# Parked parts, per-pair activation parts and a reversed second half in three down projections

## The chip, the cores and the metric

The kernel runs on one core of a Trainium2 chip. The engines that matter are TensorE (PE, matrix products; its weight loads are a row of their own), VectorE (DVE, elementwise work), ScalarE (ACT, copies and activation functions), GpSimd (POOL) and SyncE (SP). SP and POOL issue transfers between the device memory (HBM) and the on-chip memory (SBUF); 16 DMA engines carry them. Matrix products accumulate in eight PSUM banks of 128 x 512 fp32. The metric is the device time of one execution in microseconds, the median of several runs. The kernel before takes 2493.71 us (three runs, 2493.4 to 2493.81).

## What is computed

A trunk of two post-norm layers on x of 256 positions and 2048 features, all in float32. Each sub-layer is `x <- LayerNorm(ALPHA * x + sublayer(x))`.

1. A gated MLP (gMLP): `z = gelu(x @ w_in)` with 2 x 6144 columns, halves u and v; v is normalised, mixed over positions in 128-wide windows by masked 128 x 128 matrices, and `(u * s) @ w_out` projects 6144 back to 2048. This last product is the first down projection.
2. A gated feed-forward block: `h = x @ w_up` with 2 x 5504 columns, a causal width-3 convolution, `silu(g) * a`, then `@ w_down` from 5504 to 2048: the second down projection.
3. Latent attention (MLA) with 16 heads, low-rank query and key/value, rotary keys, and an output product.
4. A second feed-forward block, as 2: the third down projection.

## The kernel before

**Numbers and splits.** An fp32 product is made of three products in fp32r. A tensor x becomes a high part (ACT's rounding copy) and a low part (DVE's subtraction), and `prod_b` issues high x high, low x high and high x low, each a matmul of 512 columns on a 128 x 128 weight tile. `prod_a` does the same in the up and gate stages with the weights on the other side.

**The stream of weights.** `Feed` holds one list of chunks, in the order in which PE uses them: 48 chunks of the v stage, 48 of the gate stage u, the first down projection, the first up stage, and so on. A chunk is 128 x 2048 fp32 (1.05 MB). `Feed._load` issues its load on SP's queue into a slot `raw`; `Feed._split` makes the parts `wh` and `wl`. `Feed.next` hands out a chunk and first issues the splits of two chunks ahead and the loads of four. All of these, the activations, the residual and the parts live in one pool `big` of 22 slots of 8 KB per partition; a load waits until its slot is released. The order of the instructions on each engine is set when the program is built, by a scheduler that issues each as soon as it expects its inputs; afterwards every engine works through its list in order.

**Eight and seven products.** In the v stage and the down projections a chunk is a unit of two k (two 128-row blocks of the contraction) by 1024 output columns, and x has two blocks of 128 positions: a 2 x 2 by 2 x 2 block product. `Banks.eight` forms it as eight block products. `Banks.seven` forms it in the manner of Strassen and Winograd as seven, from sums of weight blocks (`ts`, split to `th`, `tl`, by `Feed._seven`) and sums of activation blocks (`combine`). Four of the eight banks (`q3`, `p2`, `e`, `q4`, called DIRECT) take direct terms; the other four (OWN) are joined by `Banks.rest` after the last seven of a half and added to the residual by `Norm.fold`; `Norm.piece` adds DIRECT.

**A down projection.** `down` goes twice over all k, once for each half of the 2048 output columns. `BACK` lists which units take seven products (7 of 24 in each half of the first down projection, 6 of 22 in the others) and the order of the second half. The activations' parts are made four k at a time by `Sums.quad`, and the sums of a seven by `Sums.make`. The last units of the second half are held back (`late`) and worked off in `boundary`, between the parts of the layer norm. The residual occupies two slots throughout; `Norm.restore` brings it back to its scaled form during the next up stage from rows that `Norm.rows` loads.

**Stages in time.** v up to 257 us of the profiled execution, u to 549, the first down projection to about 803, the first up stage to 1285, its down projection to about 1511, attention to about 1773, the second up stage to 2255, and the last down projection to the end. In an up stage a group is four chunks and two pairs of columns; its epilogue (`conv`, `pair`) runs on ACT and DVE while PE is at the next group.

Of the kernel before, what the change touches and what calls it, by code (L numbers as in the profile page):

```python
# [15 lines left out]
P = 128  # L16
# [32 lines left out]
V_PAIRS = [[0, 1, 2, 3, 4, 5, 6, 7]] + [[2, 0, 3, 1, 4, 5, 6, 7]] * 5  # L49
V_SEVEN = [()] + [(2, 3, 4, 6)] * 5  # L50

# [8 lines left out]
def halves(n_k):  # L60

    one = [tuple(range(k, min(k + 2, n_k))) for k in range(0, n_k, 2)]
    two = []
    for q in BACK[n_k][1]:
        two += one[2 * q : 2 * q + 2][:: -1 if q in BACK[n_k][2] else 1]
    return [one, two]


class Feed:
# [3 lines left out]
    def __init__(self, nc, pool, chunks):  # L73
        self.nc, self.pool, self.chunks = nc, pool, chunks
        self.raw, self.parts = {}, {}
        self.loaded = self.split = self.used = 0

    def _load(self):
        ap, cols = self.chunks[self.loaded][:2]
# [14 lines left out]
    def _split(self):  # L94
        i = self.split
        cols, kind = self.chunks[i][1:]
# [36 lines left out]

    def ahead(self, n_load, n_split):
# [15 lines left out]
def trunk(ctx: ExitStack, tc: tile.TileContext, x, xT, gm_in, gm_wout, ffn_up, ffn_dn,  # L150
# [7 lines left out]
    ps = ctx.enter_context(tc.tile_pool(name="ps", bufs=8, space=bass.MemoryType.PSUM))  # L158

# [10 lines left out]
    chunks = []  # L170
# [6 lines left out]
    def back(w, n_k):  # L177

        for hf, units in enumerate(halves(n_k)):
            c = slice(hf * 1024, (hf + 1) * 1024)  # L180
            for u in units:
                if len(u) == 1:
                    chunks.append((w[u[0], :, c], 1024, "wide"))
                else:
                    chunks.append((w[u[0] : u[0] + 2, :, c].rearrange("k p c -> p k c"), 2048,
                                   "seven" if u[0] in BACK[n_k][0] else "wide"))

# [11 lines left out]
    feed = Feed(nc, big, chunks)  # L199

    idle = cpool.tile([P, 512], BF16, name="idle")
# [6 lines left out]

    def combine(name, o, k1, k2):


        t = tp.tile([P, 4, P], F32, tag="t2", name=f"xs{name}", bufs=6)
        b0, b1 = slice(0, P), slice(P, S)
        nc.vector.tensor_tensor(t[:, 0], k1[:, b1], k2[:, b1], ALU.subtract)
        nc.vector.tensor_tensor(t[:, 1], t[:, 0], k1[:, b0], ALU.subtract)
        nc.vector.tensor_tensor(t[:, 2], k1[:, b0], k1[:, b1], ALU.subtract)
        nc.vector.tensor_tensor(t[:, 3], k2[:, b0], t[:, 1], ALU.add)
# [3 lines left out]
        return [(o[:, 0, i], o[:, 1, i]) for i in range(4)]  # L221
# [40 lines left out]
    ones = cpool.tile([P, P], F32, name="ones")  # L262
    nc.gpsimd.memset(ones, 1.0)
# [45 lines left out]
    def sum_halves(acc, name):  # L309
        lo = tp.tile([P, S], F32, tag="t1", name=f"lo_{name}", bufs=8)  # L310
        nc.scalar.copy(lo, acc[:, S : 2 * S])  # L311
        h = tp.tile([P, S], F32, tag="t1", name=f"h_{name}", bufs=8)
# [3 lines left out]
    def split_act(src, name):  # L316

        t = tp.tile([P, 2 * S], F32R, tag="t2", name=name, bufs=6)
# [11 lines left out]
    class Banks:  # L330
# [17 lines left out]
        def seven(self, a, sums, wh, wl, th, tl):  # L348
            s1, s2, s3, s4 = sums
            self.to("p1", a[0][0], wh, wl, 0)  # L350
            self.to("q5", s1, th, tl, 0)
            self.to("p7", s3, th, tl, 512)
            self.to("p6", s2, th, tl, 1024)
            self.to("q3", s4, wh, wl, 512)
            self.to("p2", a[0][1], wh, wl, 1024)
            self.to("q4", a[1][1], th, tl, 1536)

        def rest(self):

            acc = self.acc  # L360
            p1, u2, u3, w, d = [tp.tile([P, 512], F32, tag="t2", name=f"{self.tag}{n}", bufs=6)
# [5 lines left out]
            nc.vector.tensor_tensor(d, w, acc["p7"], ALU.subtract)  # L367
            return w, p1, d, u3

    class Sums:  # L370

# [786 lines left out]
```

## Time and profile before

| | |
|---|---|
| median of three runs | 2493.71 us |
| the profiled execution, its own time | 2493.04 us |
| its span | 2491.3 us |
| PE busy | 2475.7 us (99%), 13028 matmuls with transposes |
| DVE busy | 1908.8 us (77%) |
| ACT busy | 1388.8 us (56%) |
| granted TensorE clock | 0.999 |
| moved by DMA | 480.27 MB, mean 193 GB/s |

The page of the profile gives busy times by engine, DMA queues, the chain of waits that ended last and the costliest groups of instructions. In a group row stand the line, the engine, the operation, what it writes and reads, its shape and count, then busy time and the mean of one in ns, then the idle time of the engine just before and what ended it. In a row by windows stand the stretch, the busy time and count of PE, its weight loads, DVE, ACT and POOL, the granted clock, the DMA share and GB/s. In a row of waits stand the engine and line that waited, the one that ended it, the total in us, how often and the longest.

### The profile page before, as it was taken

What the parts mean: (1) busy time and instruction counts of PE and PEld (TensorE: products, weight loads), DVE (VectorE), ACT (ScalarE), POOL (GpSimd) and SP (SyncE); (2) the same over time, 40 slices, a digit from 0 to 9 for tenths busy, and PEclk for the clock granted to TensorE, in tenths of its full rate; (3) what the DMA queues carried; (4) which work ended last, traced back from release to release, by engine and by line L of the source; (5) the groups of instructions that cost most, each with busy time, mean ns of one, the idle gap of its engine ahead of it and who ended that gap; (6) DMA issues with size and microseconds to landing.
All of it is one profiled execution on the core that took longest, in us unless ns stands there. A gap on an engine that the chain in (4) does not pass through costs nothing.

```text
span 2491.3 us, 32651 instructions
## 1 busy us (share of the span) xinstructions
PE 2475.7 (99%) x13028; PEld 2128.3 (85%) x13028; DVE 1908.8 (77%) x2553; ACT 1388.8 (56%) x1891; POOL 2.9 (0%) x17
## 2 busy tenths in 40 slices
PE   9999999999999999999999999999999999999998
PEld 7888888888888888888888888988888888888886
DVE  7999866678888777666778997866487676669897
ACT  6566544445565755554655566565565555546553
POOL 0000000000000000000000000000000000000000
PEclk9999999999999999999999999999999999999999
DMA  7555554555566655555546674444465455555554
GB/s 295 198 187 214 196 186 157 181 196 194 186 217 222 223 186 200 188 184 185 187 155 201 219 247 169 168 153 168 156 231 191 169 202 182 180 179 179 209 192 181
DMA packets 86456, 480.27 MB, mean 193 GB/s; under 512 B 7712, under 2 KB 8480, under 8 KB 46752
## 3 DMA queue, kind: packets, MB, share of 16 engines
q1 hardware_dynamic: 86304, 478.19, 54.4%
q8 instruction: 102, 1.67, 0.3%
q14 instruction: 50, 0.41, 0.1%
HBM read 476.07 MB, written 2.10 MB: 192 GB/s over the span
## 4 chain that ended last, share of the span: by engine, by line
PE 96%; DVE 2%; issue 1%; DMA 1%; ACT 0%; SPq 0%; DVEq 0%; ACTq 0%
PE up L167 37%; PE u L167 11%; PE dn_q L167 9%; PE dn_p L167 6%; PE wo_q L167 4%; PE v_q L167 4%; PE mo L167 4%; PE dn_e L167 3%; PE v_p L167 3%; PE wo_p L167 3%; PE upf L167 2%; PE wo_e L167 2%; PE v_e L167 1%; PE mkv L167 1%; PE kn L167 1%; PE mq L167 1%
## 5 line engine op out<-in xcount | busy, mean ns | idle before, releaser
L108 DVE TENSOR_TENSOR wl<-raw,wh 128x1024 fp32r<-128x1024 f32 (+3 forms) x651 | 899.8, 1407 | 158.6 <-ACT wh L107 115.5
L107 ACT CAST wh<-raw 128x1024 fp32r<-128x1024 f32 (+3 forms) x651 | 761.8, 1201 | 284.9 <-DVE wl L108 120.4
L167 PE MATMUL up<-xhl,wh 128*128 128x512 f32 x2624 | 611.0, 390 | 0.0
L167 PEld LDWEIGHTS up<-xhl,wh 128*128 128x128 f32 x2624 | 487.4, 188 | 97.8
L167 PEld LDWEIGHTS up<-xhl,wl 128*128 128x128 f32 x2624 | 325.8, 192 | 6.4
L167 PE MATMUL up<-xhl,wl 128*128 128x256 f32 x2624 | 328.1, 283 | 0.0
L115 ACT CAST th<-ts 128x1536 fp32r<-128x1536 f32 x116 | 121.1, 1051 | 118.6 <-DVE ts L122 103.9
L167 PE MATMUL u<-xhl,wh 128*128 128x512 f32 x768 | 183.8, 393 | 0.3 <-DVE h_u L313 0.2
L167 PEld LDWEIGHTS u<-xhl,wh 128*128 128x128 f32 x768 | 141.3, 188 | 30.8 <-PE s L167 2.1
L116 DVE TENSOR_TENSOR tl<-ts,th 128x1536 fp32r<-128x1536 f32 x116 | 138.6, 1219 | 5.3 <-ACT th L115 4.5
L115 ACT CAST wh<-raw 128x1536 fp32r<-128x1536 f32 x58 | 85.9, 1480 | 43.2 <-DMA raw<-in_ffn_dn_dram 15.2
L116 DVE TENSOR_TENSOR wl<-raw,wh 128x1536 fp32r<-128x1536 f32 x58 | 101.6, 1752 | 5.4 <-ACT wh L115 5.4
L167 PEld LDWEIGHTS u<-xhl,wl 128*128 128x128 f32 x768 | 95.6, 192 | 2.0
L167 PE MATMUL u<-xhl,wl 128*128 128x256 f32 x768 | 96.7, 283 | 0.0
L167 PE MATMUL mo<-wh,oT 128*128 128x512 f32 x256 | 82.9, 404 | 0.0
L122 DVE TENSOR_TENSOR ts<-ts,raw 128x512 f32<-128x512 f32 x116 | 79.8, 688 | 1.8
L167 PE MATMUL wo_q<-wh,woa 128*128 128x512 f32 x256 | 78.8, 389 | 0.0
L122 DVE TENSOR_TENSOR ts<-raw 128x1024 f32<-128x1024 f32 x58 | 70.8, 1220 | 4.6 <-PE u L167 1.6
L313 DVE TENSOR_TENSOR h_0a<-up,lo_0a 128x256 f32<-128x256 f32 x41 | 17.3, 421 | 72.7 <-ACT lo_0a L311 72.7
L313 DVE TENSOR_TENSOR h_1a<-up,lo_1a 128x256 f32<-128x256 f32 x41 | 17.3, 421 | 71.9 <-ACT lo_1a L311 71.9
L167 PE MATMUL dn_q<-wh,dn0a 128*128 128x512 f32 x232 | 71.7, 390 | 0.0
L167 PE MATMUL dn_q<-wh,dn1a 128*128 128x512 f32 x232 | 71.5, 389 | 0.0
(497 smaller groups left out, 3924.6 us busy)
## 6 DMA issues: line engine op xcount, KB each, us to landing
raw<-in_ffn_up_dram SPq DMA_DIRECT2D x172, 1024.0 KB, 4.7
raw<-in_gm_in_dram SPq DMA_DIRECT2D x93, 1024.0 KB, 4.7
raw<-in_ffn_dn_dram SPq DMA_DIRECT2D x84, 1024.0 KB, 5.1
raw<-in_gm_wout_dram SPq DMA_DIRECT2D x48, 1024.0 KB, 5.2
raw<-in_ml_out_dram SPq DMA_DIRECT2D x16, 1024.0 KB, 4.8
raw<-in_ml_b_dram SPq DMA_DIRECT2D x14, 1024.0 KB, 4.8
raw<-in_ml_kv_dram SPq DMA_DIRECT2D x5, 864.0 KB, 4.4
lng<-in_ln_rows_dram SPq DMA_DIRECT2D x4, 1024.0 KB, 5.0
```

Source lines behind the costliest of these rows:

```text
L107: self.nc.scalar.copy(hi[:, c], raw[:, c])
L108: self.nc.vector.tensor_tensor(lo[:, c], raw[:, c], hi[:, c].bitcast(F32), ALU.subtract)
L115: self.nc.scalar.copy(hi, raw)
L116: self.nc.vector.tensor_tensor(lo, raw, hi.bitcast(F32), ALU.subtract)
L122: add = lambda o, a, b: self.nc.vector.tensor_tensor(o, a, b, ALU.add)
L167: nc.tensor.matmul(o, l, r, start=start, stop=stop, skip_group_check=True)
L313: nc.vector.tensor_tensor(h, acc[:, 0:S], lo, ALU.add)
```

## The change

`PLAN` replaces `BACK`. It lists the units of each half in order, each with its kind: e (eight products), s (seven, parts made on demand as before) or p (seven, parked). The first down projection has 7 s and 4 p in the first half, 6 s and 4 p in the second; the other two 6 s and 7 p, then 5 s and 6 p. The second half goes backwards through k.

A parked unit is prepared during the stage ahead of its down projection. `park_all` works through the parked units, one step after each chunk of the gate stage (from the second group) or the up stage (from the third): load the unit, form the sums, split and store the weights' parts, split and store the sums' parts. The four parts go to device memory from POOL's queue, and `Feed._load` fetches them, also by POOL's queue, in place of a load and a split.

`Acts` replaces `Sums`: the parts of the activations are made for each unit of two k, three units ahead, kept for the next five entries of the plan, and made again in the second half. The residual is loaded one half at a time, eight units before a half ends; `Norm.park` stores it from POOL's queue in the up stage, and `restore` runs in four up groups instead of eight, with short row loads. The pool `big` has 23 slots; small pools shrink (8 to 6 and 6 to 5 buffers), and some constants move into pools. `seven` takes its products in another order, with those of `wh` and `wl` first, and the pairs of the v stage are reordered.

```diff
-BACK = {NF_GM: ((4, 10, 16, 22, 28, 34, 40), (11, 1, 2, 0, 4, 5, 7, 8, 10, 3, 6, 9), (5, 8)),
-        NF_FF: ((4, 10, 16, 22, 30, 34), (10, 1, 2, 0, 4, 5, 7, 8, 3, 6, 9), ())}
+PLAN = {NF_GM: ("0e 1e 2s 3e 4p 5s 6e 7e 8s 9p 10e 11s 12e 13p 14s 15e 16e 17s 18p 19e 20s 21e 22e 23e",
+                "23e 22s 21e 20p 19e 18s 17p 16e 15s 14e 13p 12s 11e 10e 9s 8p 7e 6s 5e 4e 3e 2e 1e 0e"),
+        NF_FF: ("0e 1e 2s 3p 4e 5s 6p 7e 8s 9p 10e 11s 12p 13e 14s 15p 16e 17s 18p 19e 20p 21e",
+                "21e 20p 19e 18p 17s 16e 15p 14s 13e 12p 11s 10e 9p 8s 7e 6p 5s 4e 3e 2e 1e 0e")}
...
     def _load(self):
+        if kind == "parked":
+            self.parts[self.loaded] = self._fetch(self.loaded)
+            self.loaded += 1
+            return
...
+    def park(self, i):
...
+        def store(n, t, cols):
+            d = self.dram.tile([P, cols], F32, tag=f"kept{n}{i}", name=f"kept{n}{i}", bufs=1)
+            self.nc.gpsimd.dma_start(d, t[:, 0:cols].bitcast(F32))
+            kept[n] = d
+        ap = self.chunks[i][0]
+        raw = tile("praw", F32)
+        self.nc.sync.dma_start(raw.rearrange("p (k c) -> p k c", k=ap.shape[1]), ap)
+        yield
+        t = tile("pts", F32)
+        add(two(t, 0), two(raw, 512), raw[:, None, 0:512].to_broadcast([P, 2, 512]))
+        add(t[:, 1024:1536], t[:, 0:512], raw[:, 1024:1536])
+        add(t[:, 1536:2048], t[:, 1024:1536], raw[:, 1536:2048])
+        yield
+        for n, src, o, cols in (("w", raw, 512, 1536), ("t", t, 0, 2048)):
+            hi, lo = tile(f"p{n}h", F32R), tile(f"p{n}l", F32R)
+            self._cast(hi[:, 0:cols], lo[:, 0:cols], src[:, o : o + cols])
+            store(f"{n}h", hi, cols)
+            store(f"{n}l", lo, cols)
...
+    def _fetch(self, i):
+        got = []
+        for n in ("wh", "wl", "th", "tl"):
+            d = self.kept[i].pop(n)
+            t = self.pool.tile([P, 2048], F32R, tag="big", name=f"f{n}{i}")
+            self.nc.gpsimd.dma_start(t[:, 0 : d.shape[1]], d)
+            got.append(t)
+        return got
...
-    big = ctx.enter_context(tc.tile_pool(name="big", bufs=22))
+    big = ctx.enter_context(tc.tile_pool(name="big", bufs=23))
...
+    class Acts:
+        def make(self, u, kind):
+            if u in self.got and (kind == "wide" or self.got[u][1]):
+                return
...
+                t = tp.tile([P, 4, P], F32, tag="t2", name=f"{name}t", bufs=T2)
+                turn(t, x[:, 0], x[:, 1])
+                nc.scalar.copy(flat[0][:, 4:8], t)
+                nc.vector.tensor_tensor(flat[1][:, 4:8], t, flat[0][:, 4:8].bitcast(F32), ALU.subtract)
...
+            nc.scalar.copy(hi, x)
+            nc.vector.tensor_tensor(lo, x, hi.bitcast(F32), ALU.subtract)
...
+    def park_all(until):
+        for i in [i for i in parked if feed.used < i < until]:
+            yield from feed.park(i)
+            yield
...
             for c in range(KD // nk):
                 hi, lo = feed.next()
                 prod_a(acc, xhl, range(nk * c, nk * c + nk), hi, lo)
+                if gi > 1:
+                    next(jobs, None)
...
-            if 3 <= gi < 11:
-                ln.restore((gi - 3) // 4, (gi - 3) % 4)
+            if 1 < gi < 6:
+                old.restore(gi - 2)
+            if gi in (4, 6):
+                old.park(gi // 2 - 2)
```

More of the change, by code (lines that the diff above doesn't have):

```diff
@@ L412, in down @@
+    def down(n_k, src, tag, ln, acts, skew=SKEW):
         ln.begin()
-        quads, sevens = sums.quads, BACK[n_k][0]
-        late = []
-        for hf, units in enumerate(halves(n_k)):
+        seq = plan(n_k)
+        line = seq[0] + seq[1]
+        late, at = [], 0
+        for hf, units in enumerate(seq):
             n = len(units)
-            last = [u for u in units if u[0] in sevens][-1]
+            last = [u for u, kind in units if kind != "wide"][-1]
             acc = Banks(f"{tag}{hf}", OWN + DIRECT if hf else DIRECT + OWN)
-            for i, u in enumerate(units):
+            for i, (u, kind) in enumerate(units):
@@ L429, in down @@
                     ln.prep()
[L430 to L431 removed]
+                a, sums = acts.got[u]
                 if left < skew:
                     late.append((a, *got))
[L434 to L435 removed]
+                elif kind == "wide":
+                    acc.eight(a, *got)
+                else:
+                    acc.seven(a, sums, *got)
                     if u == last:
```

279 lines of the change are left out of this document (145 added, 134 removed).

## The prediction

> **What bounds the kernel now.** I read the page's head first, then PE's waits, then the chain of waits for the pace of the work.
>
> ```profile
> span 2491.3 us, 32651 instructions
> ...
> PE 2475.7 (99%) x13028; PEld 2128.3 (85%) x13028; DVE 1908.8 (77%) x2553; ACT 1388.8 (56%) x1891; POOL 2.9 (0%) x17
> ...
> q1 hardware_dynamic: 86304, 478.19, 54.4%
> ```
> ```profile
> PE wo_q L167 <- DVE wl L108: 1.1, 1, 1.1
> PE v_p L167 <- ACT wh L107: 1.0, 1, 1.0
> ```
> ```profile
> 305.55 1.78 PE s L167 x16
> 307.83 22.04 PE u L167 x126
> ...
> 834.95 450.10 PE up L167 x2592
> 1289.14 2.72 PE dn_q L167 x12
> ...
> 1493.18 5.44 PE dn_q L167 x24
> ```
>
> PE leaves 15.6 us of the span idle, and its longest wait inside a down projection is 1.1 us. So PE's own work sets the time, and in the chain of waits that work runs at one pace: 24 matmuls of 512 columns take 5.44 us, 0.2267 us each. That is the price of a matmul here; the mean of 390 ns in the group rows is its length in the pipeline. The up stage is a bound of 128 matmuls per group, 450.10 x 128 / 2592 = 22.23 us. A group of the gate stage u lasts 22.24 + 1.78 and a gap of about a quarter, 24.3 us. One profiled execution is the base: span 2491.3, its own time 2493.04; the median of the runs is 2493.71, 0.03% above.
>
> **The change part by part.**
>
> *Fewer matmuls.* A unit of two k costs 24 matmuls as eight products and 21 as seven. Before, 14 units of the first down projection and 12 in each of the other two took seven products, 38 in all; after, 21 + 24 + 24 = 69. So 31 x 3 = 93 matmuls go (12,898 become 12,805 in the built programs), 93 x 0.2267 = **21.1 us** off the path, if PE still finds its operands. The changed orders inside a unit, of the v pairs and of the second half change no count.
>
> *Parking's work on DVE.* Of the 69 units, 34 are parked: 8 in the gate stage, 13 in each up stage. Their sums and splits move there, one unit per group.
>
> ```profile
> L108 DVE TENSOR_TENSOR wl<-raw,wh 128x2048 fp32r<-128x2048 f32 x119 | 271.4, 2288 | 33.5 <-ACT wh L107 31.1 <-PE dn_q L167 1.0 <-ACT th L115 0.8
> L116 DVE TENSOR_TENSOR wl<-raw,wh 128x1536 fp32r<-128x1536 f32 x58 | 101.6, 1752 | 5.4 <-ACT wh L115 5.4
> L122 DVE TENSOR_TENSOR ts<-ts,raw 128x512 f32<-128x512 f32 x116 | 79.8, 688 | 1.8
> L122 DVE TENSOR_TENSOR ts<-raw 128x1024 f32<-128x1024 f32 x58 | 70.8, 1220 | 4.6 <-PE u L167 1.6 <-DMA raw<-in_gm_wout_dram 1.1 <-DMA raw<-in_ffn_dn_dram 1.0
> ```
> ```profile
> 1019.12 9.16 DVE L108 TENSOR_TENSOR wl<-raw,wh 128x1024 fp32r<-128x1024 f32 x8
> ```
> ```profile
> 258.00:549.00 291.00, 290.67 (x1731) 257.50 (x1730) 199.07 (x369) 136.05 (x211) 0.00 (x0) 1.00 0.51 179
> 834.00:1285.00 451.00, 451.00 (x2602) 399.54 (x2601) 314.87 (x483) 247.60 (x373) 0.00 (x0) 1.00 0.54 189
> 1289.00:1402.00 113.00, 113.00 (x500) 93.59 (x499) 100.27 (x101) 63.72 (x54) 0.28 (x2) 1.00 0.58 193
> ```
>
> A parked unit costs DVE 1.22 + 2 x 0.69 + 1.75 + 2.29 = 6.64 us. Back to back, eight rows of 1.22 take 9.16 us, so each overlaps the next by some 0.08: 6.2 us net. In an up group DVE works 314.87 / 451 x 22.23 = 15.5 us, about 0.5 of it the restoring of the residual (sixteen steps of 0.6 over the 20 groups). So 15.0 + 6.2 = 21.2 of 22.23 us in groups 2 to 14, 95%. Groups 2 to 5 also hold the whole restore, now 4 x 0.6 us each: 23.6 us, an excess of 1.4 us a group, 5.5 us in all. Splits run two units ahead of PE (11 us), so this is covered; without that cover it would cost 5.5 us a layer. The gate stage comes to 199.07 / 291 x 24.3 + 6.2 = 22.8 of 24.3 us. DVE already held 100.27 of 113 us in a down half, 89%, with no wait of PE but the 1.1, so these shares are near what it is seen to carry, and I price them at nothing. ACT gets about 3.4 us per parked unit (its 1536 and 2048 wide copies), 55% to 70% in an up group: nothing.
>
> *Activations' parts per pair of k.* In the down stages DVE gains the four small differences and one split for every seven (67 against 19 units) and loses the on-demand splitting of the parked ones (6.8 us for each that had been an on-demand seven, 2.3 for a former eight). Over a half both sums lie within a few per cent of the 89% above: nothing, with the same cover.
>
> *Parking's traffic.* Each parked unit stores 128 x (2 x 1536 + 2 x 2048) x 4 B = 3.67 MB from POOL's queue, and is fetched in four transfers by the same queue. This is 250 MB more on 480. The trace holds no such store or fetch and no POOL transfer at all; the nearest rows are SP's loads when the queue is full, and the last stores.
>
> ```profile
> 10.00:40.00 30.00, 29.94 (x132) 24.30 (x131) 26.65 (x38) 20.96 (x22) 0.00 (x0) 1.00 1.02 422
> ```
> ```profile
> raw<-in_ffn_up_dram SPq DMA_DIRECT2D x172, 1024.0 KB, 4.7
> ...
> out_dram<-res SPq DMA_DIRECT2D x8, 256.0 KB, 2.2
> ```
>
> An up group with a parked unit moves four loads, the parked unit's load and its stores: 5 x 1.05 + 3.67 = 8.9 MB in 22.23 us, 401 GB/s against the 422 seen in the first 30 us (share 1.02, all engines full). With the restore's rows (8 x 0.26 MB) and the parking of the residual (2 x 1.05), thirteen groups move 120 MB in 289 us, 415 GB/s: all but full, with backlog carried by the slots. The gate stage needs 8.9 MB in 24.3 us, 367. The first half of an FFN down projection has 8 eights and the odd k (half an eight), 6 sevens and 7 parked: 14.5 x 1.05 + 7 x 3.67 + 1.05 for the residual = 42.0 MB in 8.5 x 5.44 + 13 x 4.76 = 108.1 us, 388 GB/s; the second half (10.5, 5 and 6) 39.3 MB in 109.5 us. So DMA has little room left, but no debt at 422. From both sides: a gain is excluded, since DMA was not the bound; the loss runs from 0 at 422 GB/s to the whole excess at the rate that the page's first part gives, 478.19 MB at 54.4%, which is 353 GB/s (priced below). I take the end at 422, since that row is a queue kept full, as it would be here, while 353 counts the latency of lone transfers.
>
> The Trainium skill, DMA: Bandwidth & Descriptors, section Bandwidth, puts HBM at about 358 GB/s per core when both cores of a pair stream, and the ceiling of the 16 engines at 435. The first 30 us, at 422, agree with the second. By the first the sum would be about that of the rival in which DMA is the bound.
>
> *Slots and queues.* From the order of the built programs I took for every load the matmul that frees its slot, and counted from there to its first use at the pace above. Before, the shortest such lead in the down projections is 10.4 us, and it belongs to the unit where PE waited the 1.1 us. After, the shortest are 11.2 us (three loads of the gate stage) and 11.6 us (the third transfer of two fetches in each FFN down projection); the other loads of down stages have 14.3 or more, up stages 22. A fetch needs its third transfer at 11.6 us: 2.62 MB by then, 6.2 us at 422, two short loads beside it 2.5, and the tail of a landing (4.7 less 1.05 / 0.422) 2.2: 10.9. That just holds; a whole fetch late would cost 8.7. I take **1 us at each of the four, 0.5 at each of the three: 5.5 us**, near the 1.1 of the row; ends 0 and 4 x 8.7 = 35. SP's queue gains 24 short row loads and 10 loads of half a residual and loses 6 long row loads, at places with leads above 14 us: nothing. POOL's queue holds beside the 272 transfers only the residual's four. The turn of an FFN half is tighter than before, since the last seven is followed by one short unit: thirteen DVE steps of 0.6 us and one split of 1.15 lie between its last matmul and the release of the fourth bank, 9.0 us, and PE asks for that bank after 2 x 2.72 + 6 x 0.68 = 9.5: 0 to 1 us, in the range.
>
> The sum: 2493.04 - 21.1 + 5.5 = 2477.4, and 0.6 more for the medians; I say **2477 us**.
>
> **The rivals.**
>
> *It all hides*, at 2472, is the lower end of the forecast and no rival.
>
> *Partly covered, still faster (2481 to 2488).* DVE at 95% and DMA at its ceiling in the same groups, each in order behind the other, lose 4 to 7 us more per FFN layer. For it: both shares above are at their limits only here. Against: PE's loads there have leads of 22 us.
>
> *DMA becomes the bound (slower).* At 353 GB/s an up group needs 8.9 / 0.353 = 25.2 us, 3.0 more than PE's; over 26 groups 78, less 14 us of lead in each layer, 50. The down halves lose 2 x (42.0 / 0.353 - 108.1) = 22 and 2 x (39.3 / 0.353 - 109.5) = 4. So 2493 - 21 + 76 = **2548 us**. It decides from some 375 GB/s down, where 2 x (13 x (23.8 - 22.2) - 14) and 2 x (112.0 - 108.1) make up the gain. For it: long reads and writes were never mixed here. Against: 422 over 30 us.
>
> *The fetch is slow (slower).* It goes from F32 in memory to an fp32r tile, a kind that no transfer of before has. At half the rate a fetch lasts 17.4 us; with its two neighbours' loads (2.5 each) 22.4 against 15.0 us of PE for the three units, 7.4 us too much, 26 times: 2493 - 21 + 192 = **2664 us**. It decides below some 340 GB/s for a fetch. Nothing in the profile speaks for it or against it. The Trainium skill, DMA: Bandwidth & Descriptors, section SWDGE vs HWDGE vs iDMA, counts a float32r destination as a cast and gives no rate; no run here shows one.
>
> *No gain.* That the sevens do not save what they should is excluded by the pace, which is one for all products; that small losses eat it all needs 21 us over some 30 tight places.
>
> **How the numbers follow.** The forecast with its lower end (2471 to 2480) has 0.57; partly covered 0.13; within 0.2% 0.05; small losses above the gain, 2499 to 2520, 0.06; DMA the bound 0.09; slow fetch 0.10. So faster 0.70, same 0.05, slower 0.25; 0.2% is 5 us, about what a measurement of this kernel can tell. The range 2470 to 2520 leaves out the slow fetch, half of the DMA case and a little below.
>
> **What would show it.** PE's count down by 93 and its busy time by 21 us; PE's waits short, at the loads named; the DMA row of an up stage near 380 to 400 GB/s in groups 2 to 14; fetches landing within 9 to 12 us. The forecast is wrong if PE waits for wl or ts in the first up groups, or for a fetched tile in every third unit of the FFN down projections.

## The result, and the profile after

The changed kernel takes 2579.81 us (median of four runs, 2574.41 to 2588.61) against 2493.56 for the kernel before on the same chip: a ratio of 1.035, 95% interval 1.0321 to 1.0379. It is slower by 86 us where 16 us less were forecast. The profiled execution, whose span of 2586.7 us is read below, is the slowest of the four, 9 us above the median.

First the head of the profile of the changed kernel, with its DMA queues, and its row of the granted clock (span, mean clock).

```profile
span 2586.7 us, 34028 instructions
...
PE 2493.3 (96%) x12935; PEld 2132.4 (82%) x12935; DVE 2092.8 (81%) x2968; ACT 1461.1 (56%) x2021; POOL 150.0 (6%) x293
...
q1 hardware_dynamic: 90336, 482.39, 51.1%
q0 software_dynamic: 39744, 253.77, 24.9%
```
```profile
core 0: 2586.7 us, clock 0.982
```

PE has 93 matmuls less than before, as it should, and is busy 18 us longer. Its pauses (all over 0.15 us between two matmuls, summed) are 77.6 us against 3.3. And the matmuls that are left, which should take 21 us less, run 39 us slower than that: the granted clock fell from 0.999 to 0.982 in the mean. Up to the last matmul it stood at half in 15 stretches, 81.9 us in all. Of these, 17.9 us lie inside pauses, where they cost nothing; in the other 64 us a matmul takes 0.43 us and not 0.23, so some 32 of the 39 us are the clock's. (The other 7 us were not followed up.) After the last matmul come 13.8 us and not 10.5. So 74 + 39 + 3 - 21 = 95, and the span grew by 95.4. The waits of PE in the changed kernel (engine and line that waited, what ended it, total us, times, longest) name the pauses:

```profile
PE u L219 <- DVE h_u L368: 19.1, 8, 5.4
PE dn_q L219 <- DVE wl L118: 10.3, 2, 5.1
PE up L219 <- ACT wh L117: 9.5, 5, 2.6
PE dn_q L219 <- ACT dn10wx L454: 7.5, 1, 7.5
PE dn_q L219 <- ACT dn00wx L454: 7.5, 1, 7.5
PE wo_q L219 <- DVE wl L118: 6.1, 2, 4.2
```

Now by stage. The windows are cut at the first matmul of a stage (stretch and its length; busy time and count of PE, weight loads, DVE, ACT, POOL; clock, DMA share, GB/s). They are the gate stage u, the first down projection, the first up stage, its down projection, attention with the second up stage, and the last down projection; the kernel before first, the changed one second.

```profile
258.20:548.80 290.60, 290.27 (x1731) 257.23 (x1729) 198.67 (x369) 135.65 (x211) 0.00 (x0) 1.00 0.51 179
548.80:803.10 254.30, 253.12 (x1122) 208.95 (x1120) 221.73 (x213) 142.76 (x120) 0.00 (x0) 1.00 0.60 203
803.10:1284.70 481.60, 481.60 (x2755) 424.68 (x2753) 334.35 (x507) 272.04 (x421) 0.00 (x0) 1.00 0.54 191
1284.70:1511.50 226.80, 226.80 (x1005) 187.68 (x1004) 201.20 (x190) 128.03 (x109) 0.32 (x2) 1.00 0.60 202
1511.50:2254.80 743.30, 742.93 (x4327) 656.30 (x4326) 515.06 (x853) 423.27 (x731) 0.00 (x0) 1.00 0.51 181
2254.80:2491.30 236.50, 225.99 (x997) 186.68 (x995) 206.61 (x200) 121.82 (x101) 0.00 (x0) 0.98 0.54 191
```
```profile
258.60:584.30 325.70, 302.69 (x1731) 264.81 (x1729) 254.48 (x420) 166.07 (x230) 18.20 (x34) 0.96 0.75 271
584.30:846.40 262.10, 252.01 (x1099) 207.15 (x1098) 215.84 (x284) 133.57 (x144) 16.06 (x31) 0.99 0.82 290
846.40:1346.20 499.80, 486.94 (x2752) 427.29 (x2752) 417.55 (x588) 313.79 (x449) 30.86 (x58) 0.99 0.82 315
1346.20:1579.70 233.50, 224.09 (x969) 183.54 (x969) 187.03 (x258) 112.31 (x127) 25.91 (x50) 0.97 0.90 339
1579.70:2342.90 763.20, 748.77 (x4324) 659.40 (x4324) 597.54 (x934) 464.27 (x759) 30.84 (x58) 0.99 0.70 264
2342.90:2586.70 243.80, 224.13 (x960) 183.32 (x960) 191.52 (x266) 106.42 (x117) 25.61 (x48) 0.96 0.83 319
```

The gate stage lost 35 us. The down stages have 21 and twice 36 matmuls less (4.8 and 8.2 us) and are still longer: they lost 12.6, 14.9 and 15.5. The up stages lost 18 and 20, of which 7.5 each is the wait for `dn00wx` and `dn10wx` at their end. So the loss lies for the most part in places of three kinds:

1. In the gate stage PE waits for `h_u`, the step on DVE that empties a bank. Nothing in that stage lost a matmul, and the DMA engines are not full there (271 GB/s, share 0.75).
2. At the start of each FFN down projection PE stands for 7.46 us, for the activations' parts of its first unit.
3. At the turn of each FFN half PE stands for 5.13 us, for a `wl`.

To each pause comes what it leaves behind. Of the two windows of 12 us around the first long wait in the gate stage, the first holds the pause of 5.44 us, the second none:

```profile
330.00:342.00 12.00, 6.56 (x31) 5.48 (x31) 11.16 (x20) 4.51 (x7) 1.59 (x3) 0.83 0.81 279
342.00:354.00 12.00, 12.00 (x63) 10.44 (x63) 8.15 (x16) 6.88 (x11) 0.00 (x0) 0.89 0.90 325
```

The clock was at half for 6.8 us, from inside the pause into the next window; 5.7 of them lie behind the pause, so it cost 5.4 and some 2.8 more. Counted in this way the gate stage's loss of 35 us is 22.8 us of pauses and 10 for the half clock behind them, with some 2 left over; each start of an FFN down projection lost 7.5 + 2.7, each turn 5.1 + 2.5, together 36 us for the four.

**The theories.** A: the loss is a few places where the list of one engine, worked off in order, has something ahead of what PE needs. B: the transfers are at their ceiling, everything is late, and the places are only where it shows. The chain in the gate stage before that first wait reads as follows (start, us, engine, what it did, and in brackets the idle time ahead and what ended it):

```profile
326.48 1.23 DVE L148 TENSOR_TENSOR pts<-praw 128x1024 f32<-128x1024 f32 x1 [4.81 <-DMA praw<-in_gm_wout_dram]
...
333.82 1.90 ACT L125 CAST pth<-pts 128x2048 fp32r<-128x2048 f32 x1 [2.85 <-DMA keptwh<-pwh]
...
336.35 2.29 DVE L126 TENSOR_TENSOR ptl<-pts,pth 128x2048 fp32r<-128x2048 f32 x1
338.56 0.42 DVE L368 TENSOR_TENSOR h_u<-u,lo_u 128x256 f32<-128x256 f32 x1
...
339.03 2.50 PE L219 MATMUL u<-xhl,wh 128*128 128x512 f32 x5 [5.44 <-DVE h_u L368]
```

DVE stood 4.8 us for the parked unit's load. Later ACT stood 2.9 us until the store of `pwh` had landed, because `pth` needs that slot. Then `ptl` ran, and only behind it `h_u`. Both of A's causes are visible here: a late load at the head of a list, and a slot that a store holds.

### The profile page after: what moved, and what is told of

It reads as the page before. It is cut to its first block, busy times and chain, and to the rows that moved or that the text cites. A ratio compares the mean times of both kernels' runs of the same rounds, so it can differ in the third digit from the quotient of the medians.

```text
span 2586.7 us, 34028 instructions
## 1 busy us (share of the span) xinstructions
PE 2493.3 (96%) x12935; PEld 2132.4 (82%) x12935; DVE 2092.8 (81%) x2968; ACT 1461.1 (56%) x2021; POOL 150.0 (6%) x293
## 4 chain that ended last, share of the span: by engine, by line
PE 48%; issue 31%; DVE 10%; DMA 7%; ACT 2%; POOL 2%; SPq 0%; DVEq 0%; POOLq 0%; ACTq 0%
PE up L219 14%; PE dn_q L219 5%; PE dn_p L219 5%; PE v_q L219 4%; PE wo_q L219 4%; PE u L219 4%; PE wo_p L219 3%; PE v_p L219 3%; DVE wl L118 3%; DMA praw<-in_ffn_dn_dram 3%; PE v_e L219 1%; PE wo_e L219 1%; PE dn_e L219 1%; DMA fth<-keptth 1%; DMA keptwh<-pwh 1%
## 5 line engine op out<-in xcount | busy, mean ns | idle before, releaser
L118 DVE TENSOR_TENSOR wl<-raw,wh 128x1024 fp32r<-128x1024 f32 (+3 forms) x620 | 832.5, 1364 | 126.3 <-ACT wh L117 112.1
L117 ACT CAST wh<-raw 128x1024 fp32r<-128x1024 f32 (+3 forms) x620 | 702.1, 1164 | 228.3 <-DMA raw<-in_ffn_dn_dram 62.0
L219 PE MATMUL up<-xhl,wh 128*128 128x512 f32 x2624 | 617.3, 392 | 9.5 <-ACT wh L117 9.5
L219 PE MATMUL u<-xhl,wh 128*128 128x512 f32 x768 | 195.9, 408 | 21.8 <-DVE h_u L368 19.1
L126 DVE TENSOR_TENSOR tl<-ts,th 128x1536 fp32r<-128x1536 f32 x110 | 130.6, 1220 | 6.9 <-ACT th L125 6.9
L125 ACT CAST wh<-raw 128x1536 fp32r<-128x1536 f32 x55 | 81.4, 1480 | 71.6 <-DMA raw<-in_ffn_dn_dram 54.2
L148 DVE TENSOR_TENSOR pts<-praw 128x1024 f32<-128x1024 f32 x34 | 41.6, 1224 | 65.1 <-DMA praw<-in_ffn_dn_dram 38.4
L126 DVE TENSOR_TENSOR ptl<-pts,pth 128x2048 fp32r<-128x2048 f32 x34 | 77.8, 2289 | 5.2 <-ACT pth L125 5.1
L125 ACT CAST pth<-pts 128x2048 fp32r<-128x2048 f32 x34 | 64.8, 1907 | 23.0 <-DMA keptwh<-pwh 9.7
L219 PE MATMUL v_q<-wh,xhl 128*128 128x512 f32 x224 | 70.0, 393 | 2.0 <-ACT wh L117 2.0
L125 ACT CAST pwh<-praw 128x1536 fp32r<-128x1536 f32 x34 | 50.2, 1477 | 38.3 <-DVE wl L118 19.0
## 6 DMA issues: line engine op xcount, KB each, us to landing
ftl<-kepttl POOLq DMA_DIRECT2D x34, 1024.0 KB, 10.5
```

The source lines that it names most:

```text
L117: self.nc.scalar.copy(hi[:, c], raw[:, c])
L118: self.nc.vector.tensor_tensor(lo[:, c], raw[:, c], hi[:, c].bitcast(F32), ALU.subtract)
L125: self.nc.scalar.copy(hi, raw)
L126: self.nc.vector.tensor_tensor(lo, raw, hi.bitcast(F32), ALU.subtract)
L148: add = lambda o, a, b: self.nc.vector.tensor_tensor(o, a, b, ALU.add)
L219: nc.tensor.matmul(o, l, r, start=start, stop=stop, skip_group_check=True)
```

## The experiments

### Work without traffic, traffic without work

```diff
# e5_traffic
-        t = tile("pts", F32)
-        add(two(t, 0), two(raw, 512), raw[:, None, 0:512].to_broadcast([P, 2, 512]))
...
-            self._cast(hi[:, 0:cols], lo[:, 0:cols], src[:, o : o + cols])
-            store(f"{n}h", hi, cols)
-            store(f"{n}l", lo, cols)
+            store(f"{n}h", raw, cols)
+            store(f"{n}l", raw, cols)
```


> Edit: a parked unit is loaded and four stores of the same sizes go out, but from the loaded tile itself: no sums, no splits. The fetches stay, and so do the products, so the output is wrong (the parked units' parts are not formed); traffic as in the changed kernel, parking's work on DVE and ACT gone. Theory A: the gate stage falls from 325.7 to at most 298, the two up stages by 5 to 8 us each, total 2530 to 2545. Theory B: the gate stage stays above 315 and the total above 2560.


```diff
# e6_work
-            self.nc.gpsimd.dma_start(d, t[:, 0:cols].bitcast(F32))
...
-    return [[(int(t[:-1]), KINDS[t[-1]]) for t in line.split()] for line in PLAN[n_k]]
+    return [[(int(t[:-1]), KINDS[t[-1].replace("p", "e")]) for t in line.split()] for line in PLAN[n_k]]
```


> Edit: parking's loads, sums and splits are done in the same places, but nothing is stored or fetched; in the down projections the parked units are loaded and take eight products (34 x 0.68 = 23 us more for PE). So DVE's and ACT's work of parking without its traffic. Theory A in its first form (DVE's work in a burst ahead of h_u): the gate stage stays above 312 us. Theory A in its second form (DVE's list stands still because the parked unit's load lands late, 9.7 us against 5.6 before): without the stores the load lands in about 5.5 us and the gate stage falls to 293 to 303. Theory B: the gate stage returns to 291 to 293 and the up stages to 482 up to the turn. The total says little (fewer sevens).

Measured: traffic alone 2556.9 us, ratio 1.0255 (1.0239 to 1.027); work alone 2504.06, ratio 1.0045 (1.0028 to 1.0062). The gate stages of the two, traffic alone first:

```profile
259.60:562.60 303.00, 294.57 (x1731) 257.70 (x1729) 204.99 (x380) 139.36 (x214) 18.05 (x34) 1.00 0.76 291
```
```profile
258.90:556.20 297.30, 291.58 (x1730) 257.49 (x1729) 254.66 (x420) 166.43 (x231) 0.00 (x0) 1.00 0.56 198
```

All of parking's work on DVE and ACT costs the gate stage 6.7 us (DVE 86% busy; in the range of A's second form), and the whole kernel, with the rest of the change, 9.6 us (2504.06 less the 2.0 us that three sevens fewer cost, against 2492.4). All of its traffic costs the gate stage 12.4. Alone they cost 19, together 35: the other 16 come of their meeting. B falls for the gate stage: the traffic is the same, two thirds of the loss are gone. For the total of e5 my expectation was too low by 12 us, since the waits at the starts and turns of the FFN down projections stayed (7.47 and 5.13 again) and the gate stage kept 5 us more than I allowed. In e6 all of these are gone too: with no fetched units, neither the starts nor the turns hold PE up by more than 1.7 us.

### The gate stage: a late load, or held slots?

```diff
# e7_five: one more step between the parked unit's load and its sums
         self.nc.sync.dma_start(raw.rearrange("p (k c) -> p k c", k=ap.shape[1]), ap)
         yield
+        yield
         t = tile("pts", F32)
```


> Edit: parking goes over five chunks for each unit instead of four; the added step lies between the load of the parked unit and its first sum, so the load has two chunks (about 11 us) more or less twice the time to land before it stands at the head of DVE's list. Nothing else changes. Theory A, second form (DVE's list stands still behind a late load of a parked unit): DVE's waits for praw fall from 65 us to under 10, the gate stage from 325.7 to between 293 and 303, the up stages lose some us less; total 2540 to 2557. Rival (slots: the loaded tile holds its slot a chunk longer, so other loads are issued later): the gate stage stays above 312, total above 2565.

2559.61 us, ratio 1.0273 (1.0255 to 1.0291). The rows are the gate stage and the up stage without its end:

```profile
258.30:577.80 319.50, 302.16 (x1729) 264.53 (x1728) 254.65 (x420) 165.26 (x229) 17.82 (x34) 0.96 0.75 276
840.60:1323.80 483.20, 483.20 (x2752) 425.92 (x2752) 411.60 (x577) 309.95 (x441) 30.86 (x58) 1.00 0.84 323
```

The up stages are cured: not one pause up to their last matmul. The gate stage is not, and the total missed A's range: DVE's waits for `praw` fell from 26.7 to 1.5 us there, and the stage by 6 us only. In their place stand waits for a slot: a `wl` of the stream waits 7.8 us until a store of `pth` has landed, with `h_u` behind it. So the late load was a minor cause in the gate stage. For the up stages the edit leaves two readings. It gives the load more time, but it also spreads a unit's traffic over five chunks: the same parking stretch ran at 359 GB/s (share 0.93, 888 to 1180 us) and not at 383 (0.97). In the changed kernel the pauses come only late in that stretch, from 1063 us on, and e9 below parks nine units in a row at 397 GB/s with hardly a pause. A late load and a debt of transfers that grows over more groups are not told apart there.

The next four edits leave work and traffic as in e7, but for small stores and copies, and change how long a store holds a slot.

```diff
# e12_store_raw, on top of e7
-            store(f"{n}h", hi, cols)
-            store(f"{n}l", lo, cols)
+            store(f"{n}h", raw, cols)
+            store(f"{n}l", raw, cols)
```


> Edit: as the run with five chunks per parked unit, and the four stores read the loaded tile instead of the parts, which are formed as before but stored nowhere; the stored values, and so the output, are wrong. Same work on DVE and ACT, same traffic, but a part's slot is free as soon as it is formed and no longer held until its store has landed. Theory slots (in the run with five chunks a split of the stream waited 7.8 us for a slot that a store still read, and h_u stood behind that split): the gate stage falls from 319.5 us to between 292 and 302, total 2530 to 2542. Rival (traffic and DVE's work together, whatever holds the slots): the gate stage stays above 312, total 2552 to 2565.

2554.9 us, ratio 1.0247 (1.0233 to 1.0261); gate stage 311.6. The loss fell by 8 us and not by 17 or more, and the total lies in the rival's range; the expectation missed, because the loaded tile's own slot is now read by four stores. One of its three long pauses:

```profile
538.87 1.90 ACT L125 CAST pth<-pts 128x2048 fp32r<-128x2048 f32 x1 [7.45 <-DMA kepttl<-praw]
540.67 0.37 ACT L367 COPY lo_u<-u 128x256 f32<-128x256 f32 x1
540.80 2.29 DVE L126 TENSOR_TENSOR ptl<-pts,pth 128x2048 fp32r<-128x2048 f32 x1 [7.94 <-ACT pth L125]
543.01 0.42 DVE L369 TENSOR_TENSOR h_u<-u,lo_u 128x256 f32<-128x256 f32 x1
...
543.48 1.96 PE L220 MATMUL u<-xhl,wh 128*128 128x512 f32 x3 [6.74 <-DVE h_u L369]
```

A store holds the slot, ACT waits 7.45 us for it, DVE waits for ACT, `h_u` stands behind, and PE pays 6.74 us.

```diff
# e15_store_resident, on top of e7
-            self.nc.gpsimd.dma_start(d, t[:, 0:cols].bitcast(F32))
+            stays = self.stays.rearrange("p k c -> p (k c)")
+            self.nc.gpsimd.dma_start(d, stays[:, 0:cols].bitcast(F32))
...
+    feed.stays = xhl[0]
# e16_token: the same, and ahead of it
+            self.nc.gpsimd.dma_start(d[:, 0:16], t[:, 0:16].bitcast(F32))
# e17_mark: the same, and ahead of it
+            mark = self.st.tile([P, 8], F32, tag="mark", name=f"mark{n}{i}", bufs=8)
+            self.nc.vector.tensor_copy(mark, t[:, 0:8].bitcast(F32))
+            self.nc.gpsimd.dma_start(d[:, 0:8], mark)
```


> Edit: as the run with five chunks per parked unit, and the four stores read a tile of the activations that stays in its slot for the whole stage, instead of the parts, which are formed as before and stored nowhere; the stored values, and so the output, are wrong. Work on DVE and ACT and traffic as with five chunks, but no slot waits for a store at all. Theory slots (in the run whose stores read the loaded tile each gap of the gate stage still ended in a wait for a slot that a store was reading): the gate stage falls from 319.5 us to between 292 and 300, total 2528 to 2542. Rival (traffic and DVE's work together): the gate stage stays above 306, total above 2546.

> Edit: as the run with five chunks per parked unit; each of the four stores becomes a store of 16 columns of the part (64 bytes per partition), which frees the part's slot when it has landed, and behind it, ordered by the memory that both write, the full store, which reads an activation tile that stays in its slot. The stored values, and so the output, are wrong. Work on DVE and ACT and traffic as with five chunks, the stores at their places; a part's slot is held for the small store's 2 to 3 us instead of the 4 to 11 us of a full one. Theory slots: the gate stage falls from 319.5 us to between 292 and 303, the up stages stay as they are (490); total 2530 to 2544. Rival (traffic and DVE's work together): gate stage above 310, total above 2550.

> Edit: as the run with five chunks per parked unit; DVE copies 8 columns of each part into a small tile of its own (four copies per parked unit, an estimated 0.1 to 0.2 us each from the small steps of 0.16 us in the trace), that tile is stored, and behind it, ordered by the memory that both write, goes the full store, which reads an activation tile that stays in its slot. The stored values, and so the output, are wrong. Work and traffic as with five chunks, stores nearly at their places; a part's slot is free as soon as the part is formed. Theory slots: the gate stage falls from 319.5 us to between 292 and 303. Rival (traffic and DVE's work together): gate stage above 312.

e15 told nothing on the question: since its stores depended on nothing in the stage, the scheduler put those of the gate stage at the start of the program, and those of each up stage at that stage's start. It took 2613.14 us, ratio 1.0484 (1.0466 to 1.0501); a gate stage without stores, 293.1 us, is much what e6 had shown (297.3 with four chunks per unit).

e16 took 2649.54, ratio 1.0623 (1.0601 to 1.0645), and went the other way: in POOL's list the small stores stood behind full ones (POOL waited up to 13.8 us), so the slots were held longer. At the same work and traffic the gate stage grew to 348.2 us.

e17 took 2544.59, ratio 1.0211 (1.0194 to 1.0228). The gate stages of e16 and of e17, the latter up to its last matmul:

```profile
258.60:606.80 348.20, 303.23 (x1730) 265.69 (x1728) 254.62 (x420) 164.39 (x228) 35.16 (x65) 0.93 0.72 256
```
```profile
258.50:551.80 293.30, 290.77 (x1730) 257.69 (x1728) 248.42 (x444) 162.75 (x225) 34.99 (x65) 1.00 0.79 298
```

With no part's slot held by a store, the stage runs in 293.3 us at 298 GB/s, with all of the work; then follows one pause of 7.8 us, where a `wl` waits 9.9 us for the slot of the resident tile that the last store still reads (301.2 with it). So 319.5, 348.2 and 293.3 us have the same work and traffic but for the small stores and copies, and differ in how long stores hold slots: ACT and DVE together wait 39, 54 and 10 us there for a store to land, the last 10 at that pause. In the gate stage this cause is shown.

```diff
# e14_gate_four, on top of e11 (below): parked 9 18 | 17 8, one in ten chunks
+    jobs = park_all(feed.used + 48 + 2 * len(PLAN[NF_GM][0].split()), 6)
```


> Edit: as the fastest run so far, but four units of the first projection are parked (9 and 18 in the first half, 17 and 8 in the second), one in ten chunks of the gate stage; 4 x 0.68 = 2.7 us less for PE. If the density of parking in the gate stage is what costs: gate stage within 3 us of 292, total 2484 to 2489. If each parked unit costs there what it costs at full density (39 us over 8 units by the last two runs, some 28 of it in the gate stage and the rest in the first projection): 2500 to 2508.

2501.77 us, ratio 1.0044 (1.0032 to 1.0057). Gate stage 304.4: 13.8 us lost for four units, 3.5 each, and in e7 28.9 for eight, 3.6 each. The profiled execution of e14 is 7 us slower than its median, so 3.5 may be high; by the medians the four units cost 16 us against e11, 4.0 each, and the eight of e10 (below) 39, 4.9 each. Density is not the main thing. Each parked unit pays its own stall, several times the 0.68 us that its seven saves.

### The starts of the FFN down projections

```diff
# e1_early
-            if gi == 21:
+            if gi == 20:
                 for t in plan(NF_FF)[0][:2]:
                     acts.make(*t)
```


> Edit: the activations' parts of the first two units of each FFN down projection are made one up group earlier. Theory A (a few places where one engine's list puts something ahead of what PE needs): the wait of 7.46 us at the start of dn0 and dn1 goes, and with it the 10.2 us at half clock behind it, 5.1 us each: 2580 - 25 = 2555, from 2550 to 2560; the gate stage stays at 326 us. Theory B (transfers at their ceiling make everything late, and the gaps are only where it shows): PE waits at the same two places for a weight part instead, and the time stays above 2570.

2561.36 us, ratio 1.0274 (1.0255 to 1.0293): 18 us less than the changed kernel, and PE no longer waits at either start. Smaller than my 25 and just outside my range, but the place is right, and B falls there. The 25 counted half clock that lies inside the pause; 2 x (7.5 + 2.7) is 20, and the four executions of either kernel differ by 12 to 14 us. In the changed kernel the scheduler had set that work behind the last pair's `silu` on ACT, whose chain waited in turn for two splits on DVE:

```profile
1335.41 2.29 DVE L118 TENSOR_TENSOR wl<-raw,wh 128x2048 fp32r<-128x2048 f32 x1
...
1338.02 2.29 DVE L118 TENSOR_TENSOR wl<-raw,wh 128x2048 fp32r<-128x2048 f32 x1
...
1345.25 0.42 ACT L823 ACTIVATE s<-c_0g 128x256 f32<-128x256 f32 x1 [1.13 <-DVE c_0g L809]
1345.57 1.12 ACT L454 CAST dn00wx<-act 128x512 fp32r<-128x512 f32 x2
...
1346.22 0.80 PE L219 MATMUL dn_q<-wh,dn00wx 128*128 128x512 f32 x1 [7.46 <-ACT dn00wx L454]
```

In e6, with the same two splits on DVE, ACT's list has `dn00wx` ahead of these `silu`, and the pause is 1.7 us.

### The turns of the FFN halves

```diff
# e2_one_turn
-T1, T2 = 6, 5
+T1, T2 = 5, 5
...
-    st = ctx.enter_context(tc.tile_pool(name="st", bufs=4))
+    st = ctx.enter_context(tc.tile_pool(name="st", bufs=3))
...
-                t = tp.tile([P, 4, P], F32, tag="t2", name=f"{name}t", bufs=T2)
+                t = tp.tile([P, 4, P], F32, tag="t3", name=f"{name}t", bufs=1)
```


> Edit: the four small differences of a seven get one buffer of their own instead of five shared ones, so DVE's list can hold only one unit's of them ahead (the pool of small tiles gives up one buffer and the pool of statistics another, for room). Theory A: DVE does 4 of these steps and not 20 ahead of the wl that PE waits for at the turn of each FFN half; the 5.13 us there become at most 1.5 and the 6.8 us at half clock go: 2580 - 2 x 7 = 2566, from 2561 to 2571. Theory B: the weight's transfer is late anyway (ACT waited 7.5 us for it), the gap stays above 4 us and the time within 5 us of 2580.

2576.99 us, ratio 1.0338 (1.0323 to 1.0353): at this place A's cure does not help, and the time is where B put it. The small steps left DVE's list as meant, `wl` ran 1.7 us behind its `wh` (5.8 in the changed kernel), and PE waited elsewhere; in e2, at the turn of the first FFN layer:

```profile
1450.73 0.50 PE L219 MATMUL dn_q<-ftl,dn020px 128*128 128x512 f32 x1 [1.48 <-DMA ftl<-kepttl]
...
1461.14 0.79 PE L219 MATMUL dn_q<-fth,dn018px 128*128 128x512 f32 x1 [5.81 <-DMA fth<-keptth]
```

That fetch had been issued at 1441.4. In the changed kernel the 36 us around the same turn, and its queues from 1420 to 1480 us (packets, MB, share of the 16 engines):

```profile
1425.00:1461.00 36.00, 34.18 (x151) 27.90 (x150) 21.31 (x24) 12.42 (x16) 6.42 (x12) 1.00 1.06 412
```
```profile
q0 software_dynamic: 2384, 15.16, 65.8%
q1 hardware_dynamic: 1995, 7.54, 33.2%
```

All 16 engines are full. In `PLAN` the units 18 and 20 are parked on both sides of the turn, so four fetches of 3.67 MB and the residual's 1.05 stand together there. (At the first projection's turn e2 did remove the wait of 4.2 us for `wl`; there A holds.)

```diff
# e9_turn_wide
-        NF_FF: ("0e 1e 2s 3p 4e 5s 6p 7e 8s 9p 10e 11s 12p 13e 14s 15p 16e 17s 18p 19e 20p 21e",
-                "21e 20p 19e 18p 17s 16e 15p 14s 13e 12p 11s 10e 9p 8s 7e 6p 5s 4e 3e 2e 1e 0e")}
+        NF_FF: ("0e 1e 2s 3p 4e 5s 6p 7e 8s 9p 10e 11s 12p 13e 14s 15p 16e 17s 18e 19e 20e 21e",
+                "21e 20e 19e 18e 17s 16e 15p 14s 13e 12p 11s 10e 9p 8s 7e 6p 5s 4e 3e 2e 1e 0e")}
```


> Edit: in the FFN plans the units 18 and 20, which stand around the turn of the halves, take eight products instead of parked parts, in both halves (8 units in the two layers, 8 x 0.68 = 5.4 us more for PE). Theory local traffic (four fetches of 3.67 MB, the residual and loads within some 36 us keep all 16 engines full, 415 GB/s, and what PE needs comes last): the gap of 5.13 us at each turn falls under 1.5 and its half clock goes, 2 x 8.5 = 17: total 2563 to 2573. Rival (the turn's own steps on DVE, the sums' joining and the residual): the gap stays above 3 us, total 2578 to 2588.

2552.95 us, ratio 1.0239 (1.0224 to 1.0254). The wait at both turns is gone, and more fell than I had said: with 9 and not 13 parked units per layer the pauses in the up stages vanished as well, but for two of 0.9 and 0.7 us. So B holds, at the turn and for those 36 us. The edit also takes two units' sums off DVE there and adds splits; that is why I lean on e2 too.

### The sum

e10 joins the edits of e1, e7 and e9; e11 has in addition:

```diff
# e11_and_gate_wide
-PLAN = {NF_GM: ("0e 1e 2s 3e 4p 5s 6e 7e 8s 9p 10e 11s 12e 13p 14s 15e 16e 17s 18p 19e 20s 21e 22e 23e",
-                "23e 22s 21e 20p 19e 18s 17p 16e 15s 14e 13p 12s 11e 10e 9s 8p 7e 6s 5e 4e 3e 2e 1e 0e"),
+PLAN = {NF_GM: ("0e 1e 2s 3e 4e 5s 6e 7e 8s 9e 10e 11s 12e 13e 14s 15e 16e 17s 18e 19e 20s 21e 22e 23e",
+                "23e 22s 21e 20e 19e 18s 17e 16e 15s 14e 13e 12s 11e 10e 9s 8e 7e 6s 5e 4e 3e 2e 1e 0e"),
```


> Edit: three edits together: the first units' activation parts one group earlier, units 18 and 20 of the FFN plans with eight products, parking over five chunks per unit. If the losses are separate places, their savings add: 2580 - 18 - 12 - (23 to 40) = 2510 to 2527. If they are one loss that moves on, the total stays above 2535. Still slower than before (2493) in either case, by what is left at the first projection's turn and end and in the up stages.

> Edit: as the run with three edits, and no unit of the first projection is parked (8 units with eight products, 8 x 0.68 = 5.4 us more for PE). Gate stage back to 291 to 292 us. If the five chunks already cured the gate stage, this run is within 6 us of that one, slower; if parking in the gate stage and its fetches still cost more than 5.4 us there, it is faster by the difference. Total between 2498 and 2525.

e10: 2522.13 us, ratio 1.0125 (1.0108 to 1.0141), in the range for separate places. (The three savings as measured, 18.4, 20.2 and 26.9, would add to 2514; e7 and e9 both remove the pauses of the up stages.) e11 parks nothing in the gate stage either: 2488.52 (2487.96 to 2493.01), ratio 0.9985 (0.9976 to 0.9994), a shade faster than before, and below the range that I had expected. Its gate stage:

```profile
260.10:551.80 291.70, 290.30 (x1730) 257.49 (x1729) 204.04 (x380) 139.95 (x215) 0.00 (x0) 1.00 0.50 173
```

From e10 to e11 the eight parked units of the first projection cost 33.6 us net, 39 gross. The pauses at that projection's turn (4.2 us), late in its second half (1.9) and at its end (2.0 and 1.6) went with them; why parking delays its end was not tried and stays open. With 15 sevens more than the kernel before, 10.2 us should go, and 4.5 went. Two losses that no experiment touched make up most of the difference. At the start of attention PE stands 2.1 us, with 3.4 us at half clock behind it. And after the last matmul the kernel before needs 10.5 us, e11 13.7: DVE's list has four steps of the other block's norm ahead of the last addition to the residual. The last matmul and that addition, before and in e11:

```profile
2480.40 0.39 PE L167 MATMUL dn_q<-wl,dn1a 128*128 128x512 f32 x1
2480.82 0.69 DVE L559 TENSOR_TENSOR res<-res,dn_q 128x512 f32<-128x512 f32 x1 [2.35 <-PE dn_q L167]
```
```profile
2477.14 0.39 PE L220 MATMUL dn_q<-wl,dn10wx 128*128 128x512 f32 x1
2477.68 2.07 DVE L646 SCALAR_TENSOR_TENSOR res<-res,lnrs,lnb 128x512 f32<-128x512 f32 x3
...
2480.33 0.68 DVE L628 TENSOR_TENSOR res<-res,dn_q 128x512 f32<-128x512 f32 x1
```

```diff
# e13_eighteen, on top of e11
-        NF_FF: ("0e 1e 2s 3p 4e 5s 6p 7e 8s 9p 10e 11s 12p 13e 14s 15p 16e 17s 18e 19e 20e 21e",
-                "21e 20e 19e 18e 17s 16e 15p 14s 13e 12p 11s 10e 9p 8s 7e 6p 5s 4e 3e 2e 1e 0e")}
+        NF_FF: ("0e 1e 2s 3p 4e 5s 6p 7e 8s 9p 10e 11s 12p 13e 14s 15p 16e 17s 18p 19e 20e 21e",
+                "21e 20e 19e 18p 17s 16e 15p 14s 13e 12p 11s 10e 9p 8s 7e 6p 5s 4e 3e 2e 1e 0e")}
```


> Edit: as the fastest run so far (2488.5: first units early, no parking in the gate stage, units 18 and 20 of the FFN plans with eight products, five chunks per unit), but unit 18 is parked again in both halves; 4 more parked units, 4 x 0.68 = 2.7 us less for PE. If one parked unit on each side of the turn is little enough traffic: 2484.5 to 2487.5. If the turn's traffic is still the limit: the gap at the turns comes back, each 3 to 8 us, 2490 to 2502.

2490.82 us, ratio 0.9989 (0.998 to 0.9998): by its total the second case, by its pauses between the two. A pause of 1.36 us came back in each layer, and the 2.7 us were spent. That is as far as parking went.

## Why the prediction was wrong

- *Fewer matmuls*: right. 93 went, 21.1 us, and e11 keeps part of it.
- *Parking's work on DVE*, "I price them at nothing": off by at most 10 us taken alone (e6), so the cover of two units ahead held nearly. The step looked at shares of busy time, and DVE was never the bound by its share (254.48 of 325.70 us in the gate stage).
- *Slots and queues* is the step that failed most. "I took for every load the matmul that frees its slot" counted PE as the only holder of slots. The stores hold the parked parts' slots until they have landed, and not only loads wait for slots: so do the splits, in the lists of ACT and DVE, where `h_u` stands behind them. In the gate stage that was 26 of 35 us (319.5 in e7, 293.3 in e17 up to its last matmul). The parked unit's own load, at the head of DVE's list after one chunk, made some 6 us more there (e7); its part in the up stages' pauses is not told apart from the traffic's.
- *Parking's traffic*: the mean was right and the mean was the error. Groups 2 to 14 were as full as said (383 GB/s) and lost some 17 us in the two layers. "The first half of an FFN down projection" was averaged to 388 GB/s over 108 us, while the plan, read backwards in the second half, puts four fetches around the turn, 412 GB/s with nothing to spare. Some 15 us.
- *Activations' parts per pair of k*, "nothing, with the same cover": at the start of an FFN down projection there is no cover, since the stage's last epilogue is ahead on ACT. 20 us by the trace, 18 by e1.
- *The turn of an FFN half*, "0 to 1 us" for thirteen DVE steps: the work was near right, the transfers behind it were not seen.
- No step priced what a pause does to the clock, some 32 us and over a quarter of all that was lost, nor the tail behind the last matmul, 3 us.
- The sum's last step is off by a little: 2477.4 and 0.6 make 2478, not 2477. It changes nothing.
- The rivals: *DMA becomes the bound* had the right direction and the wrong place (its 50 us were to come from the up groups, which lost some 17). *The fetch is slow* is refuted: in the rows of the turn 15.16 MB of fetches took 65.8% of the engines and 7.54 MB of plain loads 33.2%, the same per MB. *No gain* was set aside because "21 us over some 30 tight places" seemed much; it was 116 us, at 30 pauses of more than half a us.

## What to carry to other kernels

When an edit adds a store from a pooled buffer, treat the store as a holder of that buffer until it lands, and ask of every instruction that waits for a buffer of the pool what stands behind it in its engine's list. Work out traffic and work over the shortest stretch in which they meet, at each turn of an order and each stage's first unit, not over a half or a stage. And price a wait of PE above 2 us at more than its length.

## What the runs showed of the hardware

The clock. The trace's own record of the granted clock has, in the changed kernel, 15 stretches at 0.5 up to the last matmul, and each lasts 3.41, 6.83 or 10.24 us. Over the profiled executions of the changed kernel and the fourteen experiments I set each pause of PE beside these stretches. Of pauses of 1.0 to 1.5 us, 6 of 69 had such a stretch beginning in them or within 4 us behind; of 1.5 to 1.8 us, 3 of 24; of 1.8 to 2.1 us, 41 of 51; of 4 us and more, all 67. Many of these are the same few places, seen again in each run. A stretch costs about half of the part that lies outside the pause: after pauses of some 2 us mostly 1.7 us, after those of 5.1 us 2.4 and after those of 7.5 us 2.7 (medians). The Trainium skill, TensorE: Matmul & The Clock Gate, section "HAM oscillation — how this bites in real kernels", puts the limit at idle gaps of some 3.4 us; the measured 2 us decide here. Its window of about 3.4 us agrees with the lengths of the stretches.

Mixed traffic. Stores together with loads ran at 383 GB/s over 296 us of the first up stage (share 0.97), fetches together with loads at 412 over 36 us at the turn. The prediction's worry, that long reads and writes together would fall to 353, is not borne out; they reach nine tenths of what loads alone reach, 422.

```profile
894.00:1190.00 296.00, 290.58 (x1656) 255.51 (x1654) 269.58 (x372) 191.03 (x255) 26.03 (x49) 0.99 0.97 383
```
